# Gate and up weights of a mixture-of-experts stage: a partition's two rows taken from adjacent rows of the matrix

## The chip, the core and the metric

The kernel runs on one core of a Trainium2 chip. The metric is the device time of one execution in microseconds (us). The engines named below are TensorE (PE in the rows; its weight loads are PEld), VectorE (DVE), ScalarE (ACT), GpSimd (POOL) and SyncE (SP). The core has 16 DMA engines that serve all DMA queues; SP's loads are in queue q1 of the rows, POOL's gathers and scatters in queue q0.

## The reference, cut to what matters

One transformer block on 512 tokens of 1024 columns in float32. After the token mixer, a router gives every token two of 16 experts, and the experts' results are added with the router's weights:

```python
def hier_moe(h, lp):
    ...
    for e in range(N_EXPERTS):
        a = jax.nn.silu(h @ lp['w_gate'][e]) * (h @ lp['w_up'][e])
        y = y + combine[..., e, None] * (a @ lp['w_down'][e])
    return y
```

`w_gate` and `w_up` are 16 x 1024 x 512, `w_down` is 16 x 512 x 1024, so a row of a gate or up matrix has 2048 bytes and a row of a down matrix 4096 bytes. In h @ w_gate[e] the 1024 rows of the matrix are summed over; the order in which they are taken is free, as long as the columns of h are taken in the same order.

## The kernel before, in words

The first half of the time goes to the token mixer. The expert stage follows; its loads begin in the mixer's part, at about 230 us. The 16 experts are taken one after the other, each at a "position". The order of positions is a list written by hand, `SEQ = [0, 1, 2, 11, 3, 8, 4, 12, 5, 9, 6, 13, 7, 10, 14, 15]`. Positions are of two kinds (`groups_of`): ten are heavy, with up to 128 tokens, and six are light, with few tokens, so that two or four pieces of the work fit side by side in TensorE's columns.

For every expert SP loads eight pieces of gate and up (`load`, L1299: kinds 0 and 1, parts 0 to 3) and four of down (kind 2), 512 KB each, into a ring of 22 raw buffers (`NRAW`). A gate or up piece holds 256 of the 1024 rows: partition p gets the rows 256*part + p and 256*part + 128 + p, two k-blocks of 128 rows. `static_w` and `dyn_w` give the source: experts at the first three positions are known when the kernel is built, the others are chosen by the number of tokens and read through a register. All loads are issued by SP in program order; a load waits until its buffer has been read.

What happens to a piece depends on the position. At a heavy one, ScalarE rounds it to a high part (`S.copy(hi.ap, r.ap)`, L1321), VectorE makes the low part from it (L1322), and TensorE does three matmuls for each k-block (`gate_up`, L1464 to L1466: high by high, low by high, high by low). At a light one TensorE reads the raw piece itself (`light_mm`, rows named gul and yl).

The tokens of an expert come by a gather that POOL issues (`fetch`, L1328): up to 128 rows of 4096 bytes of the normalised input `h2d`, into one of two buffers `xe`. TensorE turns them block by block (`turn`, L1356, heavy, rows named xet; `turn_light`, L1340, rows named xlt), 8 blocks of 128 columns for a tile, and the turned block kk is the left operand for the k-block kk of the weights. The first expert's tokens are not gathered: `own_list` (L1266) picks them by matmuls from the tokens in on-chip memory, into `xe0`. Results go back by scatters with addition (`scatter`, L1573), also POOL's. A gather can be issued only when its `xe` buffer has been turned.

The program emits the 8 transposes of a tile in one row. Which instruction comes when on each engine is settled when the kernel is built, by a scheduler that plans with estimated durations; within an engine the order is then fixed. After the last expert, a tail scales, adds and writes the output.

Of the kernel before, what the change touches and what calls it, by code (L numbers as in the profile page):

```python
# [43 lines left out]
def expert_at(p):  # L44

    return 4 * (p % 4) + p // 4
# [126 lines left out]
def bc(ap, shape):  # L173
    return ap.to_broadcast(shape)
# [5 lines left out]
def body(ctx, tc, I, C, out, dbg=None):  # L180
# [3 lines left out]
    V, S, G, PE, SP = (wrap(e) for e in (nc.vector, nc.scalar, nc.gpsimd, nc.tensor, nc.sync))  # L184
# [13 lines left out]
    def pF(name="pf"):  # L198
        return psF.tile([128, 512], F32, name=name, tag="F")

    def pA(name="pa"):
        return psA.tile([128, 512], F32, name=name, tag="A")
# [3 lines left out]
    def pT(name="pt"):  # L206
        i = turnT[0] % 2 if heldT[0] is None else 1 - heldT[0]
        turnT[0] = i + 1
        return psT[i].tile([128, 512], F32, name=name, tag="T")

    def mm(o, l, r, start, stop):
        PE.matmul(out=o, lhsT=l, rhs=r, start=start, stop=stop)  # L212
# [71 lines left out]
    ident = k1[:, 0:128]  # L284
# [20 lines left out]
    for i, nm in enumerate(("w_q", "w_k", "w_v")):  # L305
        G.dma_start(out=wst[:, 16 * i:16 * i + 16].rearrange("p (h o) -> p h o", h=4),
                    in_=I[nm].rearrange("l (h b) i o -> (l b i) h o", h=4))
    wifs = FA.get(192, "wifs")
    for i, nm in enumerate(("w_if_fwd", "w_if_bwd")):
        G.dma_start(out=wifs[:, 96 * i:96 * i + 96].rearrange("p (k j) -> p k j", k=12),  # L310
                    in_=I[nm].rearrange("l (k p) j -> p (l k) j", p=128))
# [21 lines left out]
    for i in range(3):  # L333
# [5 lines left out]
        tp = pT("bdt")  # L339
# [346 lines left out]
    for d in range(2):  # L686
        for h in range(4):
            r = 32 * d + h
# [3 lines left out]
    for t0, nt in ((0, 4), (4, 2)):  # L692
        tp = pT("colt")
# [4 lines left out]
    tp = pT("flt")  # L698
# [20 lines left out]
    for t in (4, 5, 0, 1, 2, 3):  # L719
        tp = pT("at")  # L720
# [4 lines left out]
        for h in range(4):  # L725
            l = xml[:, h, 1 + t * 128:129 + t * 128] if t < 4 else xmc[:, h, 1 + (t - 4) * 128:129 + (t - 4) * 128]
# [137 lines left out]
    for h in range(4):  # L864
# [13 lines left out]
        for d in range(2):  # L878
            r = 32 * d + h
# [56 lines left out]
        tp = pT("hT")  # L936
# [12 lines left out]
    for i, dst in enumerate((sh2c, s2c)):  # L949
        tp = pF("adc")  # L950
        n = 64 if i else 128
# [72 lines left out]
    h2b = [FA.get(1024, f"h2_{i}") for i in range(4)]  # L1024
# [122 lines left out]
    def after(eng, f):  # L1147
        if eng in line and nc.cur_bb is block:
            with tc.issue_after(line[eng].ins):
                line[eng] = f()  # L1150
        else:
            line[eng] = f()
# [79 lines left out]
    P0 = p0b.v("p (t s) -> p t s", t=4)  # L1232
    a0b = FA.get(16, "a0")
    A0 = a0b.ap.bitcast(BF16)[:, 0:4]
    xe0, xep = [], []
# [11 lines left out]
    def own_list(t0, n):  # L1247
        if not xep:
            xep.append(pF("own"))
            xe0.extend(pA("xe") for _ in range(2))  # L1250
        ts = range(t0, t0 + n)
        for t in ts:
            pp = xep[0][:, t:t + 1]
            for s in range(t):
                mm(pp, oneb, A0[:, s:s + 1], s == 0, False)
            mm(pp, trib, A0[:, t:t + 1], t == 0, True)
        for t in ts:
            put = lambda: V.scalar_tensor_tensor(P0[:, t, :], iota, xep[0][:, t:t + 1], bc(A0[:, t:t + 1], [128, 128]), op0=OP.is_equal, op1=OP.mult)
            if t0:
                after(V, put)  # L1260
            else:
                put()
        for t in ts:
            for hf in range(2):
                for c in range(4):
                    mm(xe0[hf][:, c * 128:c * 128 + 128], h2b[t][:, hf * 512 + c * 128:hf * 512 + c * 128 + 128], P0[:, t, :], t == 0 and c == 0, t == 3 and c == 3)  # L1266

    wgu = [I["w_gate"].rearrange("l e (k p) n -> (l e) p k n", p=128), I["w_up"].rearrange("l e (k p) n -> (l e) p k n", p=128)]
    wdn = I["w_down"].rearrange("l e (k p) n -> (l e) p k n", p=128)
    ux, uy, us = [0], [0], [0]  # L1270

    def next_raw():
        rawb.append(rawb.pop(0))
        return rawb[-1]
# [17 lines left out]

    def static_w(p):
        e = expert_at(p)
        return lambda kind, k0, n: (wgu[kind] if kind < 2 else wdn)[e][:, k0:k0 + n, :]

    def load(wsrc, kind, part):
        r, kk = next_raw(), 2 if kind < 2 else 1
        SP.dma_start(out=r.v("p (k n) -> p k n", k=kk), in_=wsrc(kind, part * kk, kk))  # L1299
        return r  # L1300

    def raw_unit(wsrc, kind, part):
        if (kind, part) in early:
            r = early.pop((kind, part))
            rawb.append(r)
            return r
        return load(wsrc, kind, part)
# [28 lines left out]
    def turn_light(xe, xt, g):  # L1336
        n = 128 // g
        tp = pT("xlt")
        for k in range(8):
            PE.transpose(tp[:, k * n:k * n + n], xe[0:n, k * 128:k * 128 + 128], ident[0:n, 0:n])  # L1340
        S.copy(xt[:, 0:8 * n], tp[:, 0:8 * n])
        return xt, g

# [7 lines left out]
    def turn(xe, b, turned=()):  # L1351
        xh, xl = xhb[b], xlb[b]
        for hf in range(2):
            tp = turned[hf] if turned else pT("xet")
            for q in range(0 if turned else 4):
                PE.transpose(tp[:, q * 128:(q + 1) * 128], xe[:, hf * 512 + q * 128:hf * 512 + (q + 1) * 128], ident)  # L1356
            s = slice(hf * 512, hf * 512 + 512)
            S.copy(xh[:, s], tp)  # L1358
            V.tensor_tensor(xl[:, s], tp, xh[:, s].bitcast(F32), op=OP.subtract)  # L1359
        return xh, xl  # L1360
# [6 lines left out]
    with tc.high_priority(offset=-LOW):  # L1367
        for u in range(NU):
            pre.append(((u % 2, u // 2), unit(static_w(0), u % 2, u // 2, 2)))
# [24 lines left out]
    tokens(3, 0)  # L1394
    rw.append(route(0, 2))
    own_list(0, 3)
    own_list(3, 1)
    for b in [sq, x1Tb, rpb, wrb, mhi, mlo] + wsp.pop((1, 0)):
        b.free()
    places(1, 0, 0)  # L1400
    xs0 = turn(None, 0, xe0)
    store(3)
    rw.append(route(2, 2))
# [29 lines left out]
    def gate_up(tiles, wsrc, xs=None, mid=()):  # L1433
        if xs is None:
            xs = [turn(fetch(t[0]), 0) for t in tiles]
# [157 lines left out]
    def turned():  # L1593
        c, xe = fq.pop(0)
        g = groups_of(c)
        if g > 1:
            run["nl"] += 1
            x = turn_light(xe, xtb[:, 512 * (run["nl"] % 2):512 * (run["nl"] % 2) + 512], g)
        else:
            run["nh"] += 1  # L1600
            x = turn(xe, run["nh"] % 2)
        fetch_to(run["upto"])
        return x
# [27 lines left out]
    for c in range(NPRE):  # L1631
        lsr[c] = ls[:, c, :]
    position(0, static_w(0))


# [107 lines left out]
    for e in range(1, NPRE):  # L1743
        position(e, static_w(e))

    for kk in range(4):
        early[2, kk] = load(static_w(NPRE - 1), 2, kk)
        rawb.pop()
# [41 lines left out]
    G.dma_start(out=lstx[:, 0:30], in_=exiv[0:1, 0:30])  # L1790
    dbg("ls", ls, (128, NE, 3))
    def dyn_w(ev):
        def src(kind, k0, n):
            w = wgu[kind] if kind < 2 else wdn
            return w[bass.ds(ev, 1), :, k0:k0 + n, :].rearrange("e p k n -> p (e k) n")
        return src

    for n in range(NPRE, NE):
        c = SEQ[n]
# [94 lines left out]
    with tc.If(novf > 0):  # L1894
        for i, p in enumerate(LAST):
            scatter(yob[i], iiv[:, p:p + 1])
        with tc.For_i(0, novf, 1) as x:
# [4 lines left out]
            ev = nc.values_load(lx[0:1, 1:2], engines=(mybir.EngineType.SP,), min_val=0, max_val=NE - 1)  # L1902
# [32 lines left out]
```

## Time and profile before

| | |
|---|---|
| time, median of 3 runs (lowest to highest) | 661.88 us (660.44 to 661.98) |
| profiled execution: its own time | 663.52 us |
| profiled execution: span of its instructions | 661.7 us |
| granted TensorE clock, mean over the span | 0.928 |
| DMA packets, bytes | 74774, 165.24 MB |
| gate, up and down loads | 64 of each, 512 KB each |

The span runs from the first to the last instruction of the profiled execution; 1.8 us of its own time lie outside. A share of DMA of 1.00 means that all 16 DMA engines had a packet in hand all the time (overlapping packets can make it a little more). An idle time of an engine is put down to what ended last before the engine went on. TensorE's clock is granted at one of two levels, 2.4 GHz (1.00) and 1.2 GHz (0.50).

### The profile page before, as it was taken

Reading aid. Unit: us, or ns where it says so; the run is one execution under the profiler, and the core shown is the slowest. Engines: PE = TensorE matmul, PEld = TensorE weight load, DVE = VectorE, ACT = ScalarE, POOL = GpSimd, SP = SyncE. Lnnn points to the kernel's source line nnn. Section 1 sums busy time; section 2 is a strip of 40 time slices with the busy share of each in tenths; the row PEclk is TensorE's granted clock in tenths of the full one; section 3 lists DMA queues with packets and bytes.
Section 4 is the critical chain, followed back from the end, with each engine's and each line's share of the span. In section 5 each row is a group of like instructions: output and inputs, shape, how many; then the busy total and the mean of one; then the engine's idle time right before and its main releaser. Section 6 shows DMA issues by size and latency. Waiting matters only on the chain. (4 is left out here: it accounts for less than half of the span.)

```text
span 661.7 us, 9133 instructions
## 1 busy us (share of the span) xinstructions
PE 551.9 (83%) x3073; PEld 377.5 (57%) x3073; DVE 374.2 (57%) x692; ACT 294.8 (45%) x478; POOL 223.8 (34%) x263
## 2 busy tenths in 40 slices
PE   3789979799999969995997999999968959898640
PEld 1356955697555647873874866576625526374530
DVE  3560694826157744349997896555605426285880
ACT  2460626443233425234483764555506335366630
POOL 7333850065043248236422146112120100002272
PEclk9979999899999979997898899999979979999875
DMA  9965602031799865456686799999999999996331
GB/s 270 385 226 184 231 0 66 15 96 49 238 303 314 263 256 180 145 217 224 224 292 207 253 396 367 351 369 364 368 366 394 370 365 371 387 372 248 108 128 24
DMA packets 74774, 165.24 MB, mean 250 GB/s; under 512 B 9305, under 2 KB 16757, under 8 KB 74724
## 3 DMA queue, kind: packets, MB, share of 16 engines
q1 hardware_dynamic: 66628, 154.07, 64.3%
q0 software_dynamic: 5536, 10.08, 6.4%
q10 hardware_dynamic: 2560, 0.47, 0.4%
q8 instruction: 25, 0.41, 0.2%
q14 instruction: 25, 0.20, 0.1%
HBM read 154.92 MB, written 15.02 MB: 257 GB/s over the span
## 5 line engine op out<-in xcount | busy, mean ns | idle before, releaser
L1322 DVE TENSOR_TENSOR U<-U,U 128x1024 fp32r<-128x1024 f32 x118 | 141.5, 1244 | 34.3 <-ACT U L1321 33.9
L1321 ACT CAST U<-U 128x1024 fp32r<-128x1024 f32 x118 | 118.8, 1050 | 20.9 <-PE y L212 7.0
L212 PE MATMUL y<-U,U 128*128 128x512 f32 x368 | 99.4, 409 | 10.2 <-ACT U L1503 4.3
L212 PEld LDWEIGHTS y<-U,U 128*128 128x128 f32 x368 | 69.0, 193 | 28.8 <-ACT U L1503 4.5
L212 PE MATMUL up<-U,U 128*128 128x512 f32 x188 | 57.6, 402 | 2.6 <-ACT U L1321 1.4
L212 PE MATMUL gate<-U,U 128*128 128x512 f32 x186 | 55.3, 399 | 3.4 <-ACT U L1321 2.4
L212 PE MATMUL uz<-U,U 128*128 128x512 f32 x192 | 52.6, 409 | 0.3 <-ACT U L602 0.2
L215 POOL TENSOR_TENSOR U<-U,U 128x512 fp32r<-128x512 f32 (+2 forms) x32 | 43.3, 1369 | 4.6 <-ACT U L427 1.8
L212 PE MATMUL gul<-U,U 128*32 128x256 f32 (+1 forms) x296 | 43.6, 475 | 0.0
L212 PEld LDWEIGHTS up<-U,U 128*128 128x128 f32 x188 | 34.5, 189 | 13.1 <-DVE U L1322 2.6
L1573 POOL DMA_INDIRECT ybuf<-U,U x7 | 11.9, 1694 | 89.0 <-ACT U L1553 72.2
L212 PEld LDWEIGHTS uz<-U,U 128*128 128x128 f32 x192 | 34.9, 189 | 12.3 <-issue 5.5
L212 PEld LDWEIGHTS gate<-U,U 128*128 128x128 f32 x186 | 34.0, 188 | 13.7 <-ACT U L1321 4.8
L1573 POOL DMA_INDIRECT ybuf<-U x8 | 13.9, 1733 | 80.9 <-ACT U L1549 58.2
L1359 DVE TENSOR_TENSOR U<-xet,U 128x512 fp32r<-128x512 f32 x18 | 12.1, 686 | 30.4 <-ACT U L1358 30.3
L1356 PE MATMUL xet<-U,U 128*128 128x128 f32 x72 | 13.1, 307 | 18.7 <-DMA U<-h2d,U 16.3
L1328 POOL DMA_INDIRECT U<-h2d,U x16 | 20.1, 1258 | 25.2 <-PE up L212 14.6
L212 PE MATMUL win<-U,U 128*128 128x512 f32 x96 | 26.1, 419 | 0.0
L1358 ACT CAST U<-xet 128x512 fp32r<-128x512 f32 x18 | 10.1, 586 | 34.0 <-PE xet L1356 33.9
L1356 PEld LDWEIGHTS xet<-U,U 128*128 128x128 f32 x72 | 8.6, 152 | 28.3 <-issue 20.3
L215 DVE TENSOR_TENSOR U<-U,U 128x512 fp32r<-128x512 f32 (+1 forms) x18 | 16.2, 919 | 12.5 <-POOL U L215 8.7
L427 ACT CAST U<-U 128x512 fp32r<-128x512 f32 (+2 forms) x30 | 21.1, 761 | 4.0 <-DMA U<-in_w_in_dram 4.0
(436 smaller groups left out, 1056.8 us busy)
## 6 DMA issues: line engine op xcount, KB each, us to landing
U<-in_w_gate_dram SPq DMA_DIRECT2D x64, 512.0 KB
U<-in_w_up_dram SPq DMA_DIRECT2D x64, 512.0 KB
U<-in_w_down_dram SPq DMA_DIRECT2D x64, 512.0 KB
U<-in_w_ada_dram SPq DMA_DIRECT2D x48, 512.0 KB
U<-in_w_in_dram SPq DMA_DIRECT2D x6, 1024.0 KB
U<-in_w_out_dram SPq DMA_DIRECT2D x4, 1024.0 KB
U<-in_x_dram SPq DMA_DIRECT2D x4, 512.0 KB
x0d<-U SPq DMA_DIRECT2D x4, 512.0 KB
```

The source lines that it names most:

```text
L212: PE.matmul(out=o, lhsT=l, rhs=r, start=start, stop=stop)
L215: (eng or V).tensor_tensor(o, a, b, op=OP.subtract)
L427: S.copy(hi[:, s], raw[:, s])
L1321: after(S, lambda: S.copy(hi.ap, r.ap))
L1322: after(V, lambda: V.tensor_tensor(lo.ap, r.ap, hi.ap.bitcast(F32), op=OP.subtract))
L1328: g = G.indirect_dma_start(out=xe[0:n], out_offset=None, in_=h2d[:, :], in_offset=bass.IndirectOffsetOnAxis(ap=gi[0:n], axis=0), bounds_ch ...
L1356: PE.transpose(tp[:, q * 128:(q + 1) * 128], xe[:, hf * 512 + q * 128:hf * 512 + (q + 1) * 128], ident)
L1358: S.copy(xh[:, s], tp)
L1359: V.tensor_tensor(xl[:, s], tp, xh[:, s].bitcast(F32), op=OP.subtract)
L1573: run["scatter"] = G.indirect_dma_start(out=to, out_offset=bass.IndirectOffsetOnAxis(ap=gi, axis=0), in_=yo[:, 0:n], in_offset=None, bound ...
```

## The change

A gate or up piece still holds the same 256 rows, but partition p now gets the rows 256*part + 2p and 256*part + 2p + 1, which are adjacent in memory: 4096 bytes in a row for each partition in place of twice 2048. The k-block k of piece q is then made of the rows 256*q + k, 256*q + k + 2 and so on. The columns of the tokens are taken in the same order: `cols_of` gives every second column of a stretch of 256. It is used where tokens are turned or picked: `own_list`, `turn_light` and `turn`. Down loads keep their layout; the sources in `static_w` and `dyn_w` take a part's number instead of a first block and a count.

```diff
-                    mm(xe0[hf][:, c * 128:c * 128 + 128], h2b[t][:, hf * 512 + c * 128:hf * 512 + c * 128 + 128], P0[:, t, :], t == 0 and c == 0, t == 3 and c == 3)
-    wgu = [I["w_gate"].rearrange("l e (k p) n -> (l e) p k n", p=128), I["w_up"].rearrange("l e (k p) n -> (l e) p k n", p=128)]
+                    mm(xe0[hf][:, c * 128:c * 128 + 128], h2b[t][:, cols_of(4 * hf + c)], P0[:, t, :], t == 0 and c == 0, t == 3 and c == 3)
+    wgu = [I[nm].rearrange("l e (q p k) n -> (l e) p q k n", p=128, k=2) for nm in ("w_gate", "w_up")]
+
+    def cols_of(c):
+        q, k = divmod(c, 2)
+        return slice(256 * q + k, 256 * q + 256, 2)
...
     def static_w(p):
         e = expert_at(p)
-        return lambda kind, k0, n: (wgu[kind] if kind < 2 else wdn)[e][:, k0:k0 + n, :]
+        return lambda kind, part: wgu[kind][e][:, part, :, :] if kind < 2 else wdn[e][:, part:part + 1, :]

     def load(wsrc, kind, part):
         r, kk = next_raw(), 2 if kind < 2 else 1
-        SP.dma_start(out=r.v("p (k n) -> p k n", k=kk), in_=wsrc(kind, part * kk, kk))
+        SP.dma_start(out=r.v("p (k n) -> p k n", k=kk), in_=wsrc(kind, part))
         return r
...
-            PE.transpose(tp[:, k * n:k * n + n], xe[0:n, k * 128:k * 128 + 128], ident[0:n, 0:n])
+            PE.transpose(tp[:, k * n:k * n + n], xe[0:n, cols_of(k)], ident[0:n, 0:n])
...
-                PE.transpose(tp[:, q * 128:(q + 1) * 128], xe[:, hf * 512 + q * 128:hf * 512 + (q + 1) * 128], ident)
+                PE.transpose(tp[:, q * 128:(q + 1) * 128], xe[:, cols_of(4 * hf + q)], ident)
...
     def dyn_w(ev):
-        def src(kind, k0, n):
-            w = wgu[kind] if kind < 2 else wdn
-            return w[bass.ds(ev, 1), :, k0:k0 + n, :].rearrange("e p k n -> p (e k) n")
+        def src(kind, part):
+            if kind < 2:
+                return wgu[kind][bass.ds(ev, 1), :, part:part + 1, :, :].rearrange("e p q k n -> p (e q k) n")
+            return wdn[bass.ds(ev, 1), :, part:part + 1, :].rearrange("e p k n -> p (e k) n")
         return src
```

## Rows read from the trace of the kernel before

**Rows 1.** Stages: length, busy us (instructions) by engine, clock, DMA share, GB/s.
```profile
405.00:480.00 75.00, 73.92 (x510) 47.28 (x511) 41.66 (x44) 40.26 (x56) 17.65 (x14) 1.00 1.03 364
480.00:500.00 20.00, 13.11 (x48) 4.06 (x46) 1.39 (x2) 1.97 (x4) 3.33 (x3) 0.83 1.05 370
500.00:600.00 100.00, 85.80 (x417) 51.25 (x417) 49.35 (x49) 47.33 (x61) 9.94 (x7) 0.95 1.03 377
600.00:604.00 4.00, 2.53 (x12) 0.67 (x11) 0.69 (x1) 2.01 (x3) 0.46 (x1) 1.00 0.65 263
604.00:608.00 4.00, 3.22 (x13) 2.37 (x14) 3.77 (x4) 4.00 (x6) 1.08 (x1) 1.00 0.55 143
```

**Rows 2.** Matmuls' waits, 400 to 604 us: total us, times, longest.
```profile
PE xet L1356 <- DMA U<-h2d,U: 11.7, 2, 6.0
PE xet L1356 <- DVE U L1504: 2.1, 3, 0.8
```

**Rows 3.** ScalarE's waits for weight loads, 400 to 604 us.
```profile
ACT U L1321 <- DMA U<-in_w_up_dram: 0.9, 1, 0.9
ACT U L1321 <- DMA U<-in_w_gate_dram: 0.3, 1, 0.3
```

**Rows 4.** TensorE weight-load waits for weight pieces, 400 to 604 us.
```profile
PEld gul L212 <- DMA U<-in_w_up_dram: 0.6, 2, 0.3
...
PEld yl L212 <- DMA U<-in_w_down_dram: 0.2, 1, 0.2
```

**Rows 5.** SP's issues in order of time: start, us, line, tile, count.
```profile
567.48 0.38 SPq L1299 DMA_DIRECT2D U<-in_w_up_dram  x1
...
593.23 5.13 SPq L1299 DMA_DIRECT2D U<-in_w_down_dram  x4
```

**Rows 6.** ScalarE in order of time: start, us, line, what, count.
```profile
585.22 6.74 ACT L1321 CAST U<-U 128x1024 fp32r<-128x1024 f32 x7
...
620.84 3.88 ACT L1321 CAST U<-U 128x1024 fp32r<-128x1024 f32 x4
```

**Rows 7.** Loads issued from 400 to 600 us: count, KB of one.
```profile
U<-in_w_gate_dram SPq DMA_DIRECT2D x40, 512.0 KB
```

**Rows 8.** Stages with down packets alone, then gate and up alone.
```profile
448.00:450.00 2.00, 2.00 (x12) 0.71 (x10) 0.10 (x1) 0.00 (x0) 0.13 (x1) 1.00 1.02 408
495.00:500.00 5.00, 4.53 (x20) 1.26 (x16) 0.00 (x0) 0.43 (x1) 0.00 (x0) 1.00 1.05 388
```

**Rows 9.** TensorE in order of time, transposes after a gather; in brackets the idle time.
```profile
363.18 0.66 PE L1356 MATMUL xet<-U,U 128*128 128x128 f32 x2 [3.74 <-DMA U<-h2d,U]
...
490.37 0.66 PE L1356 MATMUL xet<-U,U 128*128 128x128 f32 x2 [6.02 <-DMA U<-h2d,U]
...
536.17 1.09 PE L1356 MATMUL xet<-U,U 128*128 128x128 f32 x4 [5.67 <-DMA U<-h2d,U]
```

**Rows 10.** Gathers issued at 447.1, 481.6, 528.6 us: issue to landing.
```profile
DMA to landing us min/median/max: 7.6/7.6/7.6
...
DMA to landing us min/median/max: 8.6/8.6/8.6
...
DMA to landing us min/median/max: 7.5/7.5/7.5
```

**Rows 11.** SP's queue, 447 to 455, 481 to 491, 528 to 537: packets, MB.
```profile
q1 hardware_dynamic: 930, 2.61, 89.6%
...
q1 hardware_dynamic: 1168, 2.96, 84.9%
...
q1 hardware_dynamic: 1279, 2.52, 77.4%
```

**Rows 12.** Weight loads of the transposes and picks: count, ns minimum, median, maximum, first, last.
```profile
L1356 PEld LDWEIGHTS xet<-U,U x72: 137/140/230, 334.0 to 582.0; 128*128 128x128 f32 x72
L1340 PEld LDWEIGHTS xlt<-U,U x56: 133/137/140, 357.7 to 528.6; 32*128 32x128 f32 x32, 64*128 64x128 f32 x24
L212 PEld LDWEIGHTS xe<-U,U x64: 186/192/337, 316.2 to 326.5; 128*128 128x128 f32 x64
```

## What the change should do

> **What bounds the kernel now.** I read the stages first. From 405 to 600 us the DMA engines never rest: their share is 1.03 to 1.05 and they move 364 to 377 GB/s [rows 1]. That looks like a stage bound by its weight loads. But in the first part of it TensorE is busy 73.92 of 75 us, at full clock, and over the 100 us after 500 it is busy 85.80 [rows 1]. Two resources that are both full are told apart by who waits for whom, so the waits came next. In the 204 us from 400 to 604 TensorE's matmuls have no wait on a weight load at all. Their longest wait is for a gather of tokens, 11.7 us in two pieces of up to 6.0; the next is 2.1 us on VectorE [rows 2]. ScalarE, which rounds the heavy pieces, waits 1.2 us for weight loads in all that time [rows 3]. TensorE's weight loads, which read the light pieces raw, wait 1.5 us in four such rows, of which the largest and the smallest are shown [rows 4].
>
> The last question is where the loads stand against their readers. SP issues the last gate or up load of the last expert but one at 567.48 us, and 21 more loads of the same size stand behind it, the last four from 593.23 [rows 5]. The queue thins out from 600 on (263, then 143 GB/s) [rows 1]; if it is empty by 604 to 612, 21 loads at 1.35 us (below) put the landing of that load at 576 to 584 us. ScalarE casts it as the last of the seven from 585.22, so at about 591 [rows 6]: 7 to 15 us later. The last four loads are cast from 620.84, some 22 us after the last was issued [rows 6]. So the loads run ahead of their readers, and the end is set by TensorE's fixed order of work with the gather waits in it, and then by the tail. The loads and the readers happen to go at nearly the same pace, which is why both look full.
>
> **The change part by part.**
>
> *The packets.* Where only down packets flow (rows of 4096 bytes) the engines move 408 GB/s, where only gate and up packets flow 388 GB/s, both at a share above 1.00 [rows 8]. A load of 524288 bytes takes 1.285 us by the first and 1.351 by the second: 0.066 us saved for each gate or up load. From 400 to 600 us 40 loads of gate are issued [rows 7] and as many of up, so the stream would be done 80 x 0.066 = 5.3 us earlier. How much of it reaches the end? At most what the readers now wait for loads: 1.2 + 1.5 = 2.7 us [rows 3, 4]. At least nothing, since none of these waits comes out as an idle matmul [rows 2]. I take 0.3 us, near the lower end: the single waits are 0.2 to 0.9 us long, and TensorE is idle for only 1.1 of the 75 us after 405 [rows 1]. What hides the other 5.0 us is TensorE's own work; if a reader were right behind the loads, all 5.3 would show.
>
> *The gathers.* They share the 16 DMA engines with SP's loads, and TensorE stands still for three of them: 3.74 us until 363.18, 6.02 until 490.37, 5.67 until 536.17 [rows 9]. If an engine took packets from the two queues in turn, every gather packet would stand behind a 4096-byte packet and no longer a 2048-byte one. A load is 256 packets now and 128 then, 16 or 8 to an engine: 1.351/16 = 0.084 us against 1.285/8 = 0.161, so 0.076 us more for each. A gather of 128 rows has 8 packets to an engine, and the scatter issued just before it 8 more, so 16 x 0.076 = 1.2 us for each exposed gather, 3.7 us for three. That is the upper bound. The lower one is nothing, and rows speak for it. A gather that ran beside mixed packets (2.61 MB in 930 packets, 2.8 KB each) landed after 7.6 us, one beside gate and up packets almost alone (2.52 MB in 1279, 2.0 KB) after 7.5; one in between (2.5 KB) took 8.6 [rows 10, 11]. Going by the first two, 0.8 KB more cost 0.1 us, so 2 KB more cost 0.25. I take 0.2 us each, 0.6 us together.
>
> This is the place where a rule speaks against the change. The Trainium skill (DMA: Bandwidth & Descriptors, section "Queues, rings and completion order") says that each DMA engine goes round robin between the queues that have work, a packet at a time. By that rule it would be the 3.7 us; by the rows just named it is the 0.6. The rows do not bear the rule's full price out, but with three gathers that differ by 1.1 us among themselves they do not refute it, so it is a rival below.
>
> *The turned tokens.* Every second column is now read, 8 bytes apart, in 72 transposes for heavy tiles, 56 for light ones and 64 picks of the first expert [rows 12]. The columns are the stationary operand, so it is the weight load that may become slower. No row shows a strided one. Lower bound nothing; upper bound a doubling, 128 x 0.14 + 64 x 0.19 = 30 us with all of it on the path. The nearest row: 128 columns take 137 to 140 ns at their fastest and median in transposes, and the light tiles' loads of 32 or 64 partitions take the same 133 to 137 [rows 12], so the time hangs on the number of columns. That number stays. I take nothing. The Trainium skill (SBUF — State Buffer, section "Specifications (TRN2)") says that a read runs at full rate while at least two accesses fall into a line of 16 bytes; every second float32 does, so it gives nothing too, and no run here shows it.
>
> *The issue on SP and the tail.* An issue takes SP 0.38 us, and from 567.48 to 598.4 it issues 22 loads, one in 1.4 us [rows 5], so a shorter or longer issue changes nothing. In the tail nothing is edited.
>
> *The sum.* -0.3 + 0.6 + 0 = +0.3 us. The profiled execution took 663.52 us, 661.7 of it in its span, and would take 663.8; the median of the runs is 1.6 us below it, so I predict 662.2 us beside 661.88.
>
> **The rivals.**
>
> *The loads do set the pace* (faster). For it: a share of DMA of 1.03 and more for almost 200 us [rows 1]. Against it: no matmul waits for a load, and the late pieces lie ready for 7 to 15 us. If every load's saving came through, 5.3 us go and 0.6 come: 657.2 us. It decides from the point at which the waits for loads would be on the path for more than about 2.6 us, which is all of what rows 3 and 4 show.
>
> *Gathers behind larger packets* (slower). If the engines take the two queues' packets in turn, the three exposed gathers cost 1.2 us each, less the 0.3: 665.3 us. For it: the three waits are real, and TensorE has nothing else to do in them. Against it: the landing times in rows 10. It decides if an exposed gather grows by more than about 0.75 us. After such a wait the clock is also lower (0.83 in the stage from 480 to 500) [rows 1], which a longer wait could stretch.
>
> *The strided weight loads cost* (slower). Even a third of a doubling is 10 us: 672 us. Against it: the row that goes by columns.
>
> *The order shifts.* The scheduler plans with estimated durations, and an estimate for a load of half the packets, or for a strided read, may move instructions on engines that nobody edited. For it: the transposes of a tile, emitted eight in a row, stand in twos and fours between other matmuls [rows 9], so plans do interleave. Against it: bytes, shapes and dependences are the same. Its price is an exposed gather wait more or less, 3.7 to 6.0 us [rows 9]: about 656 or 668 us.
>
> *The change doesn't do what it says.* If the builder did not join the two rows, the packets stay at 2048 bytes: 661.9 us, with the strided reads alone.
>
> **How the numbers follow.** A measurement of this kernel tells a change from none at about 0.3%, 2 us: 659.9 to 663.9 counts as the same. Chances: my forecast 0.45; packets not joined 0.05; both lie within 0.3%, so 0.50 for the same. The loads set the pace 0.13 and a shifted order that helps 0.09: 0.22 faster. Gathers slower 0.14, a shifted order that hurts 0.10, strided loads 0.04: 0.28 slower. The range for 8 in 10 reaches from the faster rivals (657.2, 656) to the gathers' upper price and most of a lost wait: 657 to 667 us. The likeliest case's own range is 660.0 to 663.9: a gain of up to 2.7, a loss of up to 1.7.
>
> **What would show it.** Right: a stage of gate and up alone moves about 408 GB/s, there are some 16400 packets fewer (128 loads of 128), the share of DMA falls below 1.00 somewhere after 500 us because SP waits for buffers, and TensorE's waits for gathers keep to 3.7, 6.0 and 5.7 us within half a microsecond. The weight loads of xet and xlt stay at 137 to 140 ns. Wrong: xet or xlt loads above 150 ns; a gather landing 1 us later; instructions of TensorE in another order; or a span shorter by 4 us or more with the same gather waits, which would mean that the loads had been on the path where the waits did not show it.

## The result: slower by 0.7 %

The changed kernel takes 666.45 us, median of 15 runs (662.96 to 668.82), beside 661.68 us for the kernel before in the same session (15 runs, 658.17 to 664.6). The ratio is 1.0073, with a 95 % interval of 1.0052 to 1.0093. That lies inside the range that was given, but not in the likeliest case, which was no change. The profiled execution of the changed kernel took 668.0 us, 666.2 of it in its span. Of the runs below, one of filled_ordered (667.40 us, more than 1.5 % above that kernel's fastest) counts as slow and is left out of its numbers.

Line numbers are larger by 6 or 7 behind the edit (L1356 is now L1362, L1340 L1346, L1328 L1334, L1321 L1327). With line numbers set aside, the order of instructions on each of the five engines is what it was.

First the page of the changed kernel: TensorE's busy time, all packets, and SP's queue.

```profile
PE 558.3 (84%) x3073; PEld 384.6 (58%) x3073; DVE 374.0 (56%) x692; ACT 294.9 (44%) x478; POOL 224.1 (34%) x263
...
DMA packets 58390, 165.24 MB, mean 248 GB/s; under 512 B 9305, under 2 KB 16757, under 8 KB 58340
...
q1 hardware_dynamic: 50244, 154.07, 62.5%
```

There are 16384 packets fewer for the same bytes (74774 before), so the rows were joined. Then the stages of the changed kernel, with the columns of [rows 1], a stretch of weight loads alone behind them, and the 28 us around the last exposed gather.

```profile
405.00:480.00 75.00, 74.17 (x501) 48.41 (x490) 39.44 (x42) 38.12 (x54) 16.28 (x12) 1.00 1.02 371
480.00:500.00 20.00, 13.54 (x44) 4.35 (x43) 1.38 (x2) 1.72 (x4) 2.74 (x3) 0.83 1.03 380
500.00:600.00 100.00, 85.31 (x403) 52.42 (x403) 48.65 (x48) 47.34 (x61) 9.94 (x7) 0.91 0.98 361
...
495.00:500.00 5.00, 4.74 (x20) 1.35 (x16) 0.00 (x0) 0.22 (x1) 0.00 (x0) 0.95 1.03 405
...
528.00:556.00 28.00, 19.04 (x106) 11.50 (x106) 7.72 (x9) 9.39 (x13) 3.85 (x4) 0.70 0.92 344
```

The loads did become faster: 405 GB/s in a stretch that moved 388 before [rows 8], and from 500 to 600 us the DMA engines now have slack (0.98 beside 1.03 in [rows 1]). Nothing of it reached the end. The granted clock of that stage fell from 0.95 [rows 1] to 0.91, and most of that fell behind 528 us: the same 28 us of the kernel before read as follows.

```profile
528.00:556.00 28.00, 19.37 (x122) 12.38 (x123) 11.43 (x13) 13.39 (x18) 3.95 (x4) 0.82 1.03 370
```

A clock of 0.82 is 10 us of the 28 at 1.2 GHz, 0.70 is 17 us. This stretch alone doesn't tell small packets from large ones, though: it has 0.70 in all_2048 below, whose packets are small, and 0.88 in ordered_tokens, whose packets are large. Where the profiled execution lost its time is seen in TensorE's order of time. In the changed kernel:

```profile
361.50 0.68 PE L1362 MATMUL xet<-U,U 128*128 128x128 f32 x2 [4.57 <-DMA U<-h2d,U]
...
490.12 0.67 PE L1362 MATMUL xet<-U,U 128*128 128x128 f32 x2 [5.80 <-DMA U<-h2d,U]
...
537.36 1.10 PE L1362 MATMUL xet<-U,U 128*128 128x128 f32 x4 [6.02 <-DMA U<-h2d,U]
...
541.38 0.64 PE L212 MATMUL gul<-U 128*32 128x256 f32 x2
...
545.87 5.20 PE L212 MATMUL y<-U,U 128*128 128x512 f32 x14 [1.36 <-ACT U L1327]
```

The last of these in the kernel before:

```profile
543.25 3.83 PE L212 MATMUL y<-U,U 128*128 128x512 f32 x14 [1.36 <-ACT U L1321]
```

Against [rows 9] the three tiles start 1.7 us earlier, 0.25 us earlier and 1.2 us later; the y matmuls start 2.6 us later and take 1.4 us longer, at the lower clock; the span ends 4.5 us later. The lead of 1.7 us at 361 us is no gain of the change by itself: executions of one kernel differ by more (658.17 to 664.6 us above). One pair of traces can't be summed up, so the experiments have to decide.

Two groups of rows answer to the two disputed prices. The gathers issued at 481.0, 528.8 and 454.1 us, issue to landing (8.6 and 7.5 for the first two in [rows 10], 7.5 for the third in the kernel before), and below them SP's queue from 528 to 537 us, packets and MB, as the last of [rows 11]:

```profile
DMA to landing us min/median/max: 9.0/9.0/9.0
...
DMA to landing us min/median/max: 8.5/8.5/8.5
...
DMA to landing us min/median/max: 8.4/8.4/8.4
```

```profile
q1 hardware_dynamic: 726, 2.62, 72.5%
```

And the weight loads that read every second column, as [rows 12]:

```profile
L1362 PEld LDWEIGHTS xet<-U,U x72: 194/209/231, 330.9 to 586.2; 128*128 128x128 f32 x72
L1346 PEld LDWEIGHTS xlt<-U,U x56: 190/213/219, 354.7 to 529.2; 32*128 32x128 f32 x32, 64*128 64x128 f32 x24
L212 PEld LDWEIGHTS xe<-U,U x64: 194/196/337, 313.4 to 324.0; 128*128 128x128 f32 x64
```

Both suspects are alive: gathers land 0.4 to 1.0 us later, and a strided load of a transpose takes 209 to 213 ns beside 137 to 140.

### The profile page after: what moved, and what is told of

Same layout as the page of the kernel before. It is cut to its first block, busy times and chain, and to the rows that moved or that the text cites. A ratio compares the mean times of both kernels' runs of the same rounds, so it can differ in the third digit from the quotient of the medians.

```text
span 666.2 us, 9133 instructions
## 1 busy us (share of the span) xinstructions
PE 558.3 (84%) x3073; PEld 384.6 (58%) x3073; DVE 374.0 (56%) x692; ACT 294.9 (44%) x478; POOL 224.1 (34%) x263
## 5 line engine op out<-in xcount | busy, mean ns | idle before, releaser
L1328 DVE TENSOR_TENSOR U<-U,U 128x1024 fp32r<-128x1024 f32 x118 | 141.5, 1243 | 36.7 <-ACT U L1327 36.0
L1327 ACT CAST U<-U 128x1024 fp32r<-128x1024 f32 x118 | 118.8, 1050 | 21.0 <-PE pos L212 6.6
L212 PE MATMUL y<-U,U 128*128 128x512 f32 x368 | 101.3, 415 | 10.2 <-ACT U L1509 4.3
L212 PEld LDWEIGHTS y<-U,U 128*128 128x128 f32 x368 | 70.4, 197 | 29.2 <-ACT U L1509 4.5
L212 PE MATMUL gul<-U,U 128*32 128x256 f32 (+1 forms) x296 | 45.5, 495 | 0.0
L212 PEld LDWEIGHTS up<-U,U 128*128 128x128 f32 x188 | 34.5, 189 | 12.5 <-ACT U L1327 2.5
L1362 PE MATMUL xet<-U,U 128*128 128x128 f32 x72 | 14.2, 321 | 19.2 <-DMA U<-h2d,U 16.7
L1334 POOL DMA_INDIRECT U<-h2d,U x16 | 19.4, 1210 | 27.0 <-PE up L212 14.7
L1362 PEld LDWEIGHTS xet<-U,U 128*128 128x128 f32 x72 | 10.6, 207 | 28.4 <-issue 21.3
L212 PEld LDWEIGHTS gul<-U,U 128*32 128x32 f32 (+1 forms) x296 | 14.9, 128 | 15.1 <-issue 11.1
```

The lines of the kernel that those rows point to most:

```text
L1327: after(S, lambda: S.copy(hi.ap, r.ap))
L1328: after(V, lambda: V.tensor_tensor(lo.ap, r.ap, hi.ap.bitcast(F32), op=OP.subtract))
L1334: g = G.indirect_dma_start(out=xe[0:n], out_offset=None, in_=h2d[:, :], in_offset=bass.IndirectOffsetOnAxis(ap=gi[0:n], axis=0), bounds_ch ...
L1362: PE.transpose(tp[:, q * 128:(q + 1) * 128], xe[:, cols_of(4 * hf + q)], ident)
```

## The experiments

Time at half clock per run is worked out as 2 x (1 - mean granted clock) x mean span, over all runs of a kernel that entered its ratio. The gather at 528 us is the one ahead of the last exposed wait, from its issue to its landing, in the one trace of each kernel.

| kernel | median us (runs) | ratio to before, 95 % | us at half clock | gather at 528, us |
|---|---|---|---|---|
| changed kernel | 666.45 (15) | 1.0073 (1.0052 to 1.0093) | 94 | 8.5 |
| packets_alone | 664.84 (12) | 1.0056 (1.0025 to 1.0087) | 95 | 8.5 |
| stride_alone | 662.78 (12) | 1.0007 (0.9978 to 1.0036) | 87 | 7.4 |
| ordered_tokens | 664.61 (12) | 1.0047 (1.0017 to 1.0077) | 95 | 8.4 |
| stride_of_four | 671.99 (6) | 1.0171 (1.0125 to 1.0217) | 94 | 8.4 |
| all_2048 | 660.27 (12) | 1.0002 (0.9971 to 1.0034) | 91 | 7.8 |
| joined_early | 661.14 (12) | 1.0014 (0.9990 to 1.0039) | 89 | 7.5 |
| joined_late | 664.23 (8) | 1.0059 (1.0030 to 1.0088) | 94 | 8.4 |
| all_2048_correct | 668.72 (6) | 1.0147 (1.0102 to 1.0191) | 98 | not recorded |
| gate_up_1024 | 667.83 (6) | 1.0126 (1.0091 to 1.0160) | 90 | 9.1 |
| filled_before | 657.96 (12) | 0.9969 (0.9945 to 0.9993) | 73 | 7.6 |
| filled_ordered | 660.69 (11) | 1.0010 (0.9985 to 1.0035) | 77 | not recorded |

The kernel before, beside them: 661.92 us (29 runs) for the first four experiments, 660.6 (19) for the joined ones and gate_up_1024, 660.18 (29) for the rest, with 87 to 90 us at half clock.

**One half of the change at a time.** packets_alone, against the changed kernel:

```diff
     def cols_of(c):
-        q, k = divmod(c, 2)
-        return slice(256 * q + k, 256 * q + 256, 2)
+        return slice(128 * c, 128 * c + 128)
```

> The gate and up loads of the changed kernel (packets of 4096 bytes), the tokens read as before, 128 adjacent columns at a time; columns and weight rows no longer belong together, and nothing else is changed. Theory A, the strided weight loads of the token transposes make the loss (7 light tiles by 0.46 us and 18 half tiles by 0.08 us, 4.9 us with the first expert's): their cost is gone, so 661 to 662 us, a ratio of 0.998 to 1.001, xlt loads at 137 ns, xlt groups of eight back at 0.71 us. Theory B, the gathers land later behind packets of twice the size: 664 to 666 us, a ratio of 1.004 to 1.007, exposed gather waits 0.5 to 1.0 us longer than before. Theory C, no one cost but more half-clock time after 529 us, whatever starts it: a span about 4 us longer with the low stretch still ending near 543 us.

stride_alone keeps cols_of and takes the joining back:

```diff
-    wgu = [I[nm].rearrange("l e (q p k) n -> (l e) p q k n", p=128, k=2) for nm in ("w_gate", "w_up")]
+    wgu = [I[nm].rearrange("l e (q k p) n -> (l e) p q k n", p=128, k=2) for nm in ("w_gate", "w_up")]
```

> The gate and up loads of the kernel before (two packets of 2048 bytes), the tokens read in every second column as in the changed kernel; columns and weight rows no longer belong together. Theory A, strided weight loads: all of the loss is there, 665.5 to 667 us, a ratio of 1.006 to 1.008, xlt loads 213 ns and xet loads 209 ns. Theory B, gathers behind larger packets: 661 to 662.5 us, the gather waits as before (3.7, 6.0, 5.7 us). Theory C: between them, by how long the clock stays low after 529 us.

Theory A fell. The packets alone make 0.56 % of the 0.73, and the strided reads alone can't be told from nothing, though their loads in stride_alone are as slow as in the changed kernel:

```profile
L1346 PEld LDWEIGHTS xlt<-U,U x56: 190/213/218, 356.4 to 530.6; 32*128 32x128 f32 x32, 64*128 64x128 f32 x24
```

A group of eight xlt transposes takes TensorE 1.17 us instead of 0.71, and a part of that is lost in waits that were there anyway. The light tile turned just ahead of the last exposed gather makes the wait shorter, 4.99 us in stride_alone beside 5.67 in [rows 9]:

```profile
529.81 1.17 PE L1346 MATMUL xlt<-U,U 64*128 64x64 f32 x8 [0.84 <-DVE U L1365]
...
537.69 1.10 PE L1362 MATMUL xet<-U,U 128*128 128x128 f32 x4 [4.99 <-DMA U<-h2d,U]
```

**The same loads without strided reads on TensorE.** ordered_tokens reads adjacent columns and writes the tokens in another order (the core of the edit; the additions of SH2 change alike):

```diff
+    def blocks(v):
+        return v.rearrange("p (k j) -> p k j", k=2)
+    def pairs(v):
+        return v.rearrange("p (j k) -> p k j", k=2)
...
-            after(G, lambda: G.tensor_tensor(h2b[tt][:, s], x1[tt][:, s], S2[:, s], op=OP.mult))
+            after(G, lambda: G.tensor_tensor(blocks(h2b[tt][:, s]), pairs(x1[tt][:, s]), pairs(S2[:, s]), op=OP.mult))
```

> The loads of the changed kernel, and the normalised tokens written in SBUF and DRAM with the even columns of each 512 ahead of the odd ones, so that TensorE reads adjacent columns and columns and weight rows belong together; GpSimd's multiplications by the scale row (8 of 128x512), its last addition and VectorE's 7 additions of the shift row read every second element instead. Theory A: as packets_alone, 661 to 662 us, plus up to 1 us if the strided reads on GpSimd or VectorE are slower. Theory B: 664 to 666 us. Theory C: as packets_alone, since TensorE does the same.

Its transposes' weight loads are back at medians of 138 and 140 ns, and it is as slow as packets_alone. So a version of the change without its strided reads doesn't pay either, and theory B's range is the one that was met.

**A larger stride.** stride_of_four, against the changed kernel:

```diff
-        q, k = divmod(c, 2)
-        return slice(256 * q + k, 256 * q + 256, 2)
+        h, k = divmod(c, 4)
+        return slice(512 * h + k, 512 * h + 512, 4)
```

> The changed kernel with the tokens read in every fourth column of 512 instead of every second, 16 bytes apart; columns and weight rows no longer belong together. Theory A, if the price goes with the stride: xlt loads well above 213 ns (about 290 to 360), xet loads as long, and 670 to 680 us. Theory A, if the price is one for any stride: 213 ns again and 666 us. Theories B and C: 666 us whatever the loads last, since neither rests on them.

```profile
L1346 PEld LDWEIGHTS xlt<-U,U x56: 191/213/216, 358.8 to 533.0; 32*128 32x128 f32 x32, 64*128 64x128 f32 x24
...
L1362 PEld LDWEIGHTS xet<-U,U x72: 195/210/227, 334.8 to 590.1; 128*128 128x128 f32 x72
...
L212 PEld LDWEIGHTS xe<-U,U x64: 308/330/332, 310.6 to 326.5; 128*128 128x128 f32 x64
```

None of the theories expected this. The transposes' loads cost the same at 8 and at 16 bytes, but the loads of the first expert's picks, 192 ns contiguous [rows 12] and 196 at 8 bytes, jump to 330. By the first and the last start in these rows that stage takes 15.9 us, beside 10.6 in the changed kernel. That is 5.3 us more, and by the medians the kernel is 5.5 us slower than the changed one. TensorE is busy for 15.62 of the 15.9 us, so no wait inside the stage could take it up.

**Which loads?** By now the traces with joined packets had the gather at 528 us at 8.4 to 8.5 us, those without at 7.4 to 7.5. all_2048 goes the other way, against the kernel before, and splits the down loads too:

```diff
-    wdn = I["w_down"].rearrange("l e (k p) n -> (l e) p k n", p=128)
+    wdn = I["w_down"].rearrange("l e (q k p) (h n) -> (l e) p q k h n", p=128, k=2, h=2)
...
-        return lambda kind, k0, n: (wgu[kind] if kind < 2 else wdn)[e][:, k0:k0 + n, :]
+        return lambda kind, k0, n: wgu[kind][e][:, k0:k0 + n, :] if kind < 2 else wdn[e][:, k0 // 2, :, k0 % 2, :]
```

> The kernel before with its down loads, too, in packets of 2048 bytes (two rows, half the columns each; the matmuls are those of before, so columns of down end at wrong places). Theory B+C, the packet size on SP's queue sets how long a gather flies, and longer idle waits bring more half-clock time: gathers land 0.2 to 0.6 us earlier than before (under 7.4 us at 528 us, under 8.6 at 481), low clock per run no more than the 90 us of before, and 659.5 to 661.9 us, a ratio of 0.996 to 1.000, unless the stream, 0.066 us longer for each down load, gets on the path. Theory D, the loss of packets_alone has nothing to do with the size of the packets but with loads that run further ahead: the gathers keep to 8.6 and 7.5 us and the time to 661.9.

No gain, and the two gathers take 8.4 us (481) and 7.8 us (528). The one at 528 us flies beside gate and up packets of 2 KB in the kernel before as well [rows 11], so it had nothing to win, and I could have seen that. all_2048_correct, the same loads with the matmuls to match, puts TensorE's instructions in another order in 230 places and took 668.72 us (1.0102 to 1.0191); what of that is order and what packets can't be told from it.

> As all_2048, with the matmuls of down in the order that the halves ask for (six into one half's bank, then six into the other), so that the output is the reference's; VectorE and ScalarE do the same work, TensorE the same matmuls in another order. Theory B+C: as all_2048, 659.5 to 661.9 us. A shifted order could cost or give an exposed wait, 656 to 668 us. Theory D: 661.9.

joined_early and joined_late join one part of the gate and up loads each, against packets_alone. wgu2 is the layout of stride_alone; the lines shown are joined_early's, joined_late takes the two the other way round, and the dynamic loads follow suit:

```diff
     def static_w(p):
         e = expert_at(p)
+        w = wgu if p < NPRE else wgu2
```

> packets_alone with packets of 4096 bytes for the first three experts only, whose 24 gate and up loads are issued before 335 us; the other 104 in two packets of 2048 as before; tokens read as before, so columns and weight rows of the three do not belong together. Theory F, the later gathers carry the loss (in all traces so far the gather issued at 528 us takes 7.4 to 7.8 us beside packets of 2048 and 8.4 to 8.5 beside 4096, that at 455 us 7.5 against 8.5 to 9.4): gathers as in before, a ratio of 0.999 to 1.001. Theory G, the loss arises ahead of 364 us, where the filled kernels still differ: a ratio of 1.003 to 1.006.

> The other half: packets of 4096 bytes for the 104 gate and up loads from 356 us on, 2048 for the first three experts; tokens read as before. Theory F: a ratio of 1.003 to 1.006, the gathers at 528 and 455 us at 8.4 us and more. Theory G: 0.999 to 1.001 whatever the gathers do.

This settles which loads. The 104 loads from 356 us on make the loss by themselves; the 24 early ones make none that is clear of the noise, though the two intervals touch (up to 1.0039 and from 1.0030). TensorE's order in joined_late differs in ten places near 97 us, before any of these loads; stride_alone has the same ten and packets_alone none, so they don't make the difference. In joined_late the two exposed tiles in TensorE's order of time, and the landings of the gathers issued at 523 and 450 us (those of 528 and 455 before):

```profile
485.71 0.66 PE L1363 MATMUL xet<-U,U 128*128 128x128 f32 x2 [6.65 <-DMA U<-h2d,U]
...
531.86 1.09 PE L1363 MATMUL xet<-U,U 128*128 128x128 f32 x4 [7.26 <-DMA U<-h2d,U]
```

```profile
DMA to landing us min/median/max: 8.4/8.4/8.4
...
DMA to landing us min/median/max: 9.3/9.3/9.3
```

The same two views of joined_early (gathers at 527 and 453 us):

```profile
488.37 0.66 PE L1363 MATMUL xet<-U,U 128*128 128x128 f32 x2 [5.94 <-DMA U<-h2d,U]
...
534.96 1.08 PE L1363 MATMUL xet<-U,U 128*128 128x128 f32 x4 [6.35 <-DMA U<-h2d,U]
```

```profile
DMA to landing us min/median/max: 7.5/7.5/7.5
...
DMA to landing us min/median/max: 7.5/7.5/7.5
```

The two waits are 0.7 and 0.9 us longer, 1.6 together, of 3.1 us between the medians. It is not one lucky pair: in the traces with adjacent columns these waits are 5.87 to 6.02 and 5.67 to 6.35 us where the late loads are not joined (the kernel before, all_2048, joined_early) and 6.48 to 6.97 and 6.56 to 7.31 us where they are (packets_alone, ordered_tokens, joined_late).

How the 3.1 us come about is less clear. The runs of joined_late spend 94 us at half clock, those of joined_early 89. If the longer waits account for 1.6 us of the 5 and the other 3.4 have work in them, that work takes 1.7 us more: 1.6 + 1.7 = 3.3. That sum fits, but the traces don't bear it out. The stretch from the start of the light tile's transposes to the first y matmul behind the exposed tile holds the wait and most of the low clock that follows. Its length, from TensorE's order of time:

| kernel | around 490 us | around 536 us | sum |
|---|---|---|---|
| before | 19.3 | 15.1 | 34.5 |
| all_2048 | 19.1 | 16.9 | 36.1 |
| joined_early | 20.1 | 15.6 | 35.6 |
| packets_alone | 19.6 | 17.3 | 36.9 |
| ordered_tokens | 20.9 | 15.9 | 36.8 |
| joined_late | 19.4 | 17.0 | 36.4 |

The lower three, with joined late loads, are 1.3 us longer on average, waits and low clock together (the upper three differ by 1.6 among themselves), and joined_late is 0.8 us longer than joined_early. As far as six traces go, the two exposed gathers make less than half of the loss, and where the rest arises is open. The two traces can't show it: that of joined_late is its fastest run (a span of 659.6 us), that of joined_early one of its slowest (662.0).

**Smaller packets.** gate_up_1024 takes four rows and half the columns per load (the core of the edit, shown against the changed kernel; cols_of is that of packets_alone):

```diff
-    wgu = [I[nm].rearrange("l e (q p k) n -> (l e) p q k n", p=128, k=2) for nm in ("w_gate", "w_up")]
+    wgu = [I[nm].rearrange("l e (q k p) (h n) -> (l e) p q h k n", p=128, k=4, h=2) for nm in ("w_gate", "w_up")]
```

> The kernel before with gate and up loads in packets of 1024 bytes (four rows, half the columns each; columns and weight rows no longer belong together). Theory F, a gather flies longer the larger the packets beside it: the gather at 528 us takes 6.9 to 7.2 us and that at 455 us under 7.2, half of the step from 4096 to 2048; the time 659 to 661.5 us if the stream, whose rate beside such packets no run shows, stays ahead of its readers, and above 664 if it does not. Theory G: gathers at 528 us as with 2048, 7.4 to 7.8 us.

667.83 us, 1.0126 (1.0091 to 1.0160). The gather issued at 451 us (that of 455 before), beside packets mostly of 1 KB (1534 in 1.80 MB), takes 7.1 us, as theory F has it. The one at 527 us takes 9.1, which no theory has. By then the stream is late (335 GB/s from 440 to 480 us beside 361 in the kernel before, and ScalarE and VectorE wait for weight loads), and other packets fly beside this gather: 1126 in 2.53 MB, 2.2 KB on average, so 4 KB ones among those of 1 KB. The waits for weight loads from 400 to 600 us in its trace:

```profile
ACT U L1326 <- DMA U<-in_w_down_dram: 5.8, 3, 2.7
ACT U L1326 <- DMA U<-in_w_gate_dram: 2.8, 2, 2.4
DVE U L1327 <- DMA U<-in_w_up_dram: 2.1, 1, 2.1
```

**Is the half clock a cost of its own?** filled_before, against the kernel before, puts transposes that compute nothing ahead of the two exposed tiles; filled_ordered has the same lines on ordered_tokens:

```diff
             tp = turned[hf] if turned else pT("xet")
+            if hf == 0 and not turned and run["nh"] in (7, 8):
+                for f in range(40):
+                    PE.transpose(tp[:, f % 4 * 128:f % 4 * 128 + 128], ident, ident)
```

> The kernel before with 40 more transposes of the identity ahead of each of the two tiles that TensorE waits for near 484 and 530 us (into the bank that the tile's own transposes then overwrite), some 5.2 us of TensorE's work each, in the time in which it stands still. Theory C, half-clock time after the waits is a cost of its own: the low stretches at 488 and 529 us go, 17 us of low clock of which some 7.7 had work in them, so 3 to 4 us are saved: 657.5 to 659 us. Rival, the low clock costs nothing or the extra work keeps nothing up: 661.9 us or more.

> ordered_tokens (packets of 4096 bytes, tokens in blocks) with the same 80 transposes. Theory C, most of what the larger packets cost is half-clock time after these two waits: 657.5 to 659.5 us, no more than 1 us above filled_before. Theory B alone, the waits themselves cost it: 2 to 3 us above filled_before, as ordered_tokens is above before.

filled_before took 657.96 us, a ratio of 0.9969 (0.9945 to 0.9993). Both low stretches are gone; the stages with the two waits in filled_before:

```profile
475.00:495.00 20.00, 18.77 (x99) 7.86 (x97) 1.38 (x2) 2.02 (x4) 3.58 (x3) 1.00 1.04 367
520.00:540.00 20.00, 16.82 (x138) 9.53 (x135) 4.07 (x6) 6.36 (x10) 3.67 (x3) 0.99 1.02 369
```

So this kernel is faster by 2.2 us, of the 3 to 4 expected, and it is the one version here that is faster than both kernels. But it is not a test of the clock alone. The scheduler also moved real work: 24 and 28 of the light expert's gate and up matmuls, which followed the two exposed tiles in the kernel before, now run ahead of them. The first tile starts 7 us after its tokens landed (issued at 479.4, 9.2 us of flight):

```profile
495.99 0.27 PE L1359 MATMUL xet<-U,U 128*128 128x128 f32 x1
```

The stretches of the table above, in the kernel before and in filled_before:

```profile
481.81:501.15 19.34, 12.35 (x46) 4.12 (x46) 0.71 (x2) 2.54 (x5) 1.82 (x2) 0.82 1.05 370
528.13:543.25 15.12, 7.62 (x74) 3.73 (x74) 1.00 (x3) 2.80 (x6) 2.23 (x3) 0.66 1.03 366
```

```profile
479.60:497.07 17.47, 17.47 (x86) 8.13 (x86) 0.02 (x1) 1.96 (x4) 1.83 (x2) 1.00 1.04 365
524.66:538.31 13.65, 11.77 (x114) 7.36 (x114) 1.00 (x3) 2.81 (x6) 2.23 (x3) 1.00 1.01 354
```

They are 1.9 and 1.5 us shorter, by real matmuls that stepped into the waits and by the full clock, and this run can't part the two. The same move without the idle transposes was not tried. That work is slower at the lower clock is seen by itself in the y matmuls: 3.83 and 5.20 us for the same 14.

filled_ordered took 660.69 us (0.9985 to 1.0035), 2.7 above filled_before, where theory C had at most 1 and theory B 2 to 3; the two intervals overlap a little. In its trace the two stretches are as long as in filled_before, 17.47 and 13.65 us:

```profile
481.77:499.24 17.47, 17.47 (x87) 8.12 (x87) 0.02 (x1) 1.96 (x4) 1.82 (x2) 1.00 1.03 377
526.80:540.45 13.65, 11.77 (x114) 7.36 (x114) 1.00 (x3) 2.81 (x6) 2.22 (x3) 1.00 1.03 384
```

So with the waits hidden the larger packets cost nothing at these two places in the traces, and the distance in the medians has to come from somewhere else, which speaks against both theories as the whole story. The two traces run at an even distance from 364 us to the end; what the other runs of filled_ordered lose (77 us at half clock beside 73) no trace shows.

## Why the prediction was right in range and wrong in its likeliest case

**What bounds the kernel: right.** TensorE's fixed order with the gather waits in it sets the end. The loads became faster (405 GB/s, 408 forecast), the share of DMA fell below 1.00 after 500 us, and no gain came of it. Of the loads' 5.3 us I let 0.3 through; less cannot be told from it. The rival in which the loads set the pace is refuted by packets_alone.

**The gathers: the step that failed, by its size.** "I take 0.2 us each, 0.6 us together." The mechanism, its place and the upper bound of 1.2 us were on paper. The measured price at two of the three places is 0.7 and 0.9 us of wait (joined_late against joined_early). At 363 us none can be told: the waits there are 3.7 to 7.0 us in traces with small packets and 3.7 to 7.3 with large ones. What led me astray was the comparison behind the 0.2: a gather at 447 us and one at 528, two places with other work in the queues. POOL's own queue differed as well, 0.28 MB from 447 to 455 us and 0.63 MB from 528 to 537, so a small transfer beside large packets was set against a larger one beside small packets:

```profile
q0 software_dynamic: 224, 0.28, 14.2%
...
q0 software_dynamic: 431, 0.63, 26.4%
```

The gather at 447 us takes 7.5 to 7.8 us whether gate and up packets are joined or not; those at 455 and 528 us take 7.4 to 7.8 without joining and 8.4 or more with it. The same gather beside other packets would have been the right row, and the trace of before had none.

The Trainium skill (DMA: Bandwidth & Descriptors, section "Queues, rings and completion order") has the engines go round robin between queues, a packet at a time. In direction the runs bear it out. The 3.7 us that the prediction got by that rule are its own reading, though: it took each row of 2 or 4 KB in the trace for one turn, while a packet of that page holds several descriptors, typically about 9 to 17. The runs don't bear that reading out. While POOL's packets fly, from 530.7 to 536.1 us in the kernel before and from 526.0 to 531.7 us in joined_late, SP's queue moves

```profile
q1 hardware_dynamic: 606, 1.16, 61.9%
...
q1 hardware_dynamic: 417, 1.52, 66.8%
```

in packets and MB. One row to a turn would have kept the count beside as many of POOL's packets; it fell by a third, and the bytes rose by a third.

**The clock behind the waits: named, not priced.** The prediction says that a longer wait could stretch the low clock, and the sum has no term for it. The kernels whose late loads are joined spend 94 to 95 us at half clock, those without 87 to 91 (the filled ones and all_2048_correct, whose order differs, apart). That the extra low clock comes from the longer waits is argued from joined_late and joined_early and not shown; filled_before took low clock and time away together, but with real work moved into the waits, and filled_ordered speaks against the clock as the whole story.

**The strided loads: wrong in duration, nearly right in time.** "The time hangs on the number of columns" held only for contiguous columns: 209 and 213 ns, where more than 150 was to refute me. (A gather landing 1 us later was the other such sign, and the one at 528 us did, 8.5 beside 7.5.) The Trainium skill (SBUF — State Buffer, section "Specifications (TRN2)") gives full rate to two or more accesses in 16 bytes, and the same row of that page has each cross to a new line of 16 bytes pay a penalty, which the prediction left out. With the first half the traces agree for the picks (192 to 196 ns at 8 bytes, 330 at 16) and differ for the transposes, which pay some 70 ns at either stride. Their extra work on TensorE, 7 x 0.46 + 18 x 0.08 + 0.3 = 5.0 us, came out as 0.5 us by the ratio of stride_alone, with an interval from -1.5 to 2.4. One place where it goes is shown, the wait of 4.99 us that was 5.67; the rest isn't traced. The rival's 10 us was too dear by far.

**Order and joining.** No engine's order changed, and the packets were joined; both rivals are out. What came nearest is the rival with gathers behind larger packets, forecast at 665.3 us: 664.84 with the packets alone. That the numbers lie so close is partly luck, since the forecast has 1.2 us at each of three gathers, and the waits show 0.7 and 0.9 at two. The changed kernel's 666.45 has the strided loads on top, as far as the intervals let one add.

**The range: partly luck.** Its upper end of 667 us was stretched for most of a lost wait. No such wait came, and what filled that room, the strided loads and what the joined loads cost beyond 0.3 us, was not in the sum. The bounds of the likeliest case don't follow from their terms either: a gain of 2.7 us on 661.88 is 659.2, not 660.0.

**Open.** That the larger packets of the late loads make the loss is shown. How is not: the two exposed gathers land later, but their stretches hold 1.3 us of some 3, and filled_ordered keeps a distance that these places don't explain.

## What to carry to other kernels

Before making one queue's packets larger, look for small transfers on other queues that the busy engine waits for: their flight, not the stream's rate, may be what is for sale. Price such a transfer by itself beside other traffic, not by another transfer elsewhere in the kernel. And count a wait of TensorE with the low clock that follows it, and look for real work that can step into it: here that, with idle work beside it, gained 2.2 us, where shortening a hidden stream lost 3.

## What the runs showed of the hardware that was not expected

- A transpose's weight load of float32 takes 137 to 140 ns from adjacent columns and 209 to 213 ns from every second or every fourth one. The weight load of an ordinary float32 matmul takes 192, 196 and 330 ns for the three.
- The same gather took 7.1 us beside weight packets of mostly 1 KB, 7.5 beside 2 KB and 8.4 to 9.4 beside 4 KB at one place in the program (455 us). The gather at 447 us took 7.5 to 7.8 with gate and up packets of 2 or 4 KB.
- Eighty transposes that compute nothing, put ahead of two tiles with waits of 6 us, took the time from 660.18 to 657.96 us; 52 real matmuls moved into the waits with them.
